# Folding the inverses into the keys of two recurrences

## The chip, the core and the metric

The kernel runs on one core of one Trainium2 chip. The metric is the device time of one execution in microseconds (us); lower is better. A core has TensorE (matmuls, with its weight loads), VectorE, ScalarE, GpSimd (POOL) and SyncE (SP, which here issues the DMAs). Each engine runs its instructions in a fixed order and waits on semaphores for the others.

## The reference, cut to what matters

One layer of a hybrid decoder: an input projection feeds four mixers (GLA, S5, gated delta net, RWKV-7), each is gated, and an output projection with a residual and a final norm follows. A prompt of 1024 tokens and 8 single tokens with carried states go through the same weights. All is in 32-bit floats. The change touches two mixers:

```python
# gated delta net, per head, chunks of 64 tokens
tmat = low + eye                       # unit lower triangular, 64x64
sol  = triangular_solve(tmat, concat([vb, kb * exp(gc)]))
u, w = sol[..., :64], sol[..., 64:]
def step(s, inp):                      # over chunks
    v_new = uu - ww @ s
    o = qd @ s + at @ v_new
    s = gt * s + kd.T @ v_new

# RWKV-7, per head, token by token
s = s * exp(lw_t) - (s @ kk_t)[..., None] * (kk_t * a_t) + v_t[..., None] * k_t
o = s @ r_t
```

The kernel computes RWKV in chunks of 64 as well, with the same kind of triangular inverse.

## The kernel before, in words

The prompt goes through in two halves of 512 tokens (`h` = 0, 1); the second carries the 8 single tokens as well. A half has two RWKV units and two delta-net units, one for each pair of heads (`rwkv_unit`, line 377; `gdn_unit`, line 616), two GLA units, S5 and eight gates. A unit is a generator with stages: projections; preparation (decays, keys, Gram matrices `Gt`); the inverses (`inverse`, line 288: eight chunks for two heads, a loop of 62 VectorE operations, DMAs through DRAM, small products); then the recurrence over eight chunks.

The string `ORDER` (line 33) lists the stages of all units in program order, and `PRI` (line 32) lets the recurrences and inverses of RWKV and delta net go ahead of the rest. The instructions of all engines are then put in order by a planner when the kernel is built, from modelled times (line 1553); each engine follows the order that it wrote. Weights are streamed by `stream` (line 270): SP loads a tile, ScalarE and POOL split it into a high and a low part, and TensorE makes three products for each of eight rows of the input (line 278). These projections are the bulk of TensorE's work and stand between the steps of the recurrences.

A step of RWKV (lines 466 to 502) handles one chunk for two heads. `AR[:, c]` holds 64 columns of keys (`ua`) and 64 of receptances (`vk`). In a bank `pc` it adds the value part (`Gt` times values, line 488) and `AR` times the state `Sbd` (line 489); VectorE copies the key half to `r` (line 491); `XT`, the inverse, times `r` (line 494) is copied into `UV` (line 495); `Bn` times `UV` (line 496) updates the state (line 501). So the chain has three products: state, inverse, update. Delta net (lines 674 to 705) has the same chain: `KQ` times state (693), `r` by adding the scaled values `Rv` (695), `XT` times `r` (697), the copy `U` (698), `Kn` times `U` (699) and the state update (704). For each pair of chunks some transposes come first (lines 472 to 478, 680 to 684).

Buffers come from pools that rotate (`NB`, line 25): nine `ta`, six `kA` (which hold `AR`, `BK`, `KQ`, the Gram matrices of delta net and GLA, and the rows of x while `norm_x` runs), two PSUM banks `psb` and three `psc`.

Of the kernel before, what the change touches and what calls it, by code (L numbers as in the profile page):

```python
# [8 lines left out]
F32 = mybir.dt.float32  # L9
# [3 lines left out]
ALU = mybir.AluOpType  # L13
# [17 lines left out]
           rU="V", dU="V", fg="V", la="V", tlo="V", cv0="V")  # L31
# [32 lines left out]
def trunk(ctx: ExitStack, tc: tile.TileContext, I, O):  # L64
    nc = tc.nc
    V, A, G, PE, SP = nc.vector, nc.scalar, nc.gpsimd, nc.tensor, nc.sync
# [33 lines left out]
    def psb(*shape):  # L100
        return ps_b.tile(list(shape) or [128, 512], F32, tag="b", name="psb")

    def psc(*shape):
        return ps_c.tile(list(shape) or [128, 512], F32, tag="c", name="psc")

    def ta(*shape, name="ta"):
        return tmp.tile(list(shape) or [128, NH], F32, tag="ta", bufs=NB["ta"], name=name)
# [11 lines left out]
    def cp(name, out, in_, scale=None):  # L119
        if ENG[name] == "A":  # L120
            return A.copy(out, in_) if scale is None else act(out, in_, AF.Copy, scale=scale)
        if scale is None:
            return V.tensor_copy(out, in_)
        return V.tensor_scalar(out, in_, scale, None, ALU.mult)
# [20 lines left out]
    ident = cload("ident", (128, 128))  # L145
# [9 lines left out]
    i64 = cload("i64", (128, 64))  # L155
# [176 lines left out]
    inner = lambda ap: ap.rearrange("p (c f) (b t) -> p c (f b) t", f=2, b=2)[:, :, 1:3, :]  # L332
    HS = [slice(64 * h, 64 * h + 64) for h in range(2)]
    outs, gp = {}, {}
    dgp = drp.tile([8, 128, HALF], F32, name="dgp")
    dy = drp.tile([HALF, D], F32, name="dy")

    def ou_tile(m, pair, h):
        outs[m, pair, h] = un.tile([128, 4, 128], F32, tag="on", bufs=NB["on"], name=f"on{m}{pair}")
        return outs[m, pair, h]  # L340
# [36 lines left out]
    def rwkv_unit(h, pair, th):  # L377
# [71 lines left out]
        if h:  # L449
# [11 lines left out]
            SP.dma_start(out=O["rwkv_s"][pair], in_=S0)  # L461
            sample_out(mat_vec(S0, rx[:, q]), RWKV, pair)
        yield
        ou = ou_tile(RWKV, pair, h)
        V.tensor_scalar(Sbd, Sbd, fx[:, 0, 0:1], None, ALU.mult)
        for c in range(8):
            if c % 2 == 0:
                Bn = tmp.tile([128, 2, 128], F32, tag="Bn", bufs=NB["Bn"], name="Bn")
                UV = tmp.tile([128, 2, 128], F32, tag="UV", bufs=NB["UV"], name="UV")
                pt = psc(128, 4, 128)  # L470
                for j in range(2):
                    PE.transpose(pt[:, j, :], BK[:, c + j, :], ident)
                vt = [vx[:, 64 * (c + j):64 * (c + j) + 64] for j in range(2)]
                PE.matmul(pt[64:128, 2, :], vt[0], ident, start=True, stop=True)
                PE.transpose(pt[0:64, 3, :], vt[1], ident)
                A.copy(Bn, pt[:, 0:2, :])
                A.copy(UV[64:128, 0], pt[64:128, 2])
                A.copy(UV[0:64, 1], pt[0:64, 3])  # L478
            uv, bn = UV[:, c % 2, :], Bn[:, c % 2, :]
            ua, vk = HS[c % 2], HS[1 - c % 2]  # L480
            gc = lambda rows, e: Gt[c // 4][rows, c // 2 % 2 * 4 + 2 * e + c % 2]
            pc = psc()

            def mm(o, l, r, start=False):
                PE.matmul(o, l, r, start=start, stop=True, skip_group_check=True)  # L485

            for e in range(2):
                mm(pc[:, HS[e]], gc(vk, e), uv[vk, HS[e]], start=(e == 0))
            mm(pc[:, 0:128], AR[:, c, :], Sbd)
            r = tmp.tile([128, 128], F32, tag="r", bufs=NB["r"], name="r")  # L490
            cp("rr", r[ua], pc[ua, 0:128])
            cp("rS", Sbd, Sbd, fx[:, 1, c:c + 1])
            for e in range(2):
                mm(pc[ua, 128 + 64 * e:192 + 64 * e], XT[ua, c // 2 * 2 + e, :], r[ua, HS[e]])
            cp("rU", uv[ua], pc[ua, 128:256])
            mm(pc[:, 256:384], bn, uv)
            for e in range(2):
                mm(pc[vk, HS[e]], gc(ua, e)[:, vk], uv[ua, HS[e]])
            for e in range(2):
                hp = HS[e]  # L500
                V.scalar_tensor_tensor(Sbd[hp, hp], pc[hp, 256 + 64 * e:320 + 64 * e], fx[hp, 1, c:c + 1], Sbd[hp, hp], ALU.mult, ALU.add)
            A.copy(ou[ua, c // 2, :], pc[vk, 0:128])
# [113 lines left out]
    def gdn_unit(h, pair):  # L616
# [42 lines left out]
        if h:  # L659
# [10 lines left out]
            SP.dma_start(out=O["gdn_s"][pair], in_=S0)  # L670
            sample_out(mat_vec(S0, qx[:, q]), GDN, pair)
        yield
        ou = ou_tile(GDN, pair, h)
        for c in range(8):
            if c % 2 == 0:
# [14 lines left out]
            def mm(o, l, r, start=False):  # L690
                PE.matmul(o, l, r, start=start, stop=True, skip_group_check=True)

            mm(pc[:, 0:128], KQ[:, c, :], Sbd, start=True)
            r = tmp.tile([128, 128], F32, tag="r", bufs=NB["r"], name="r")
            V.tensor_tensor(r[ua], pc[ua, 0:128], rv[ua], ALU.add)
            for e in range(2):
                mm(pc[ua, 128 + 64 * e:192 + 64 * e], XT[ua, c // 2 * 2 + e, :], r[ua, HS[e]])
            cp("dU", U[ua], pc[ua, 128:256])
            mm(pc[:, 256:384], kn[ua], U[ua])
            for e in range(2):  # L700
                mm(pc[vk, HS[e]], Gt[ua, c // 2 * 2 + e, 64:128], U[ua, HS[e]])
# [855 lines left out]
```

## Time and profile before

| | |
|---|---|
| median of 3 runs | 1058.57 us (1046.91 to 1059.12) |
| the profiled execution | 1059.9 us, of which the span of the trace is 1058.1 us |
| mean granted clock of TensorE | 0.854 of 2.4 GHz |
| TensorE busy | 929.8 us, 88% of the span |
| its weight loads | 764.5 us, 72% |
| VectorE busy | 698.9 us, 66% |
| ScalarE busy | 462.4 us, 44% |
| POOL busy | 391.1 us, 37% |
| DMA | 95.91 MB, mean 91 GB/s |

Busy time of an engine is the time in which at least one of its instructions runs. Matmuls are pipelined, so TensorE counts as busy while a single matmul is in flight. The granted clock is 1.00 at 2.4 GHz and 0.50 at 1.2 GHz. A product of 32-bit floats shows as two matmul records and two weight loads; a transpose, and a product of the projections, as one.

### The profile page before, as it was taken

The numbers are of one execution on the slowest core, as the hardware profiler recorded it, in microseconds if no ns is written. First come the engines' busy times: TensorE is split into PE (matmuls) and PEld (weight loads), VectorE is DVE, ScalarE is ACT, GpSimd is POOL, SyncE is SP. The second block draws the span as 40 slices with busy tenths as digits, with TensorE's granted clock in tenths as the row PEclk, the third lists the DMA queues.
The fourth block names the chain that finished last, engine by engine and source line by source line (L and its number), as shares of the span: only waits on it lengthen the run. The fifth ranks groups of instructions, "written<-read, shape, count | busy, mean of one in ns | idle before, by whom it ended". The sixth has DMA issues, their size and how long they took to land. (4 is left out here: it accounts for less than half of the span.)

```text
span 1058.1 us, 17042 instructions
## 1 busy us (share of the span) xinstructions
PE 929.8 (88%) x5994; PEld 764.5 (72%) x5994; DVE 698.9 (66%) x1843; ACT 462.4 (44%) x1088; POOL 391.1 (37%) x439
## 2 busy tenths in 40 slices
PE   3898989899998898797999989898998989897595
PEld 2676757678777686687788868777886968685594
DVE  8627895767548645836577979888976555725523
ACT  4355625331643423531663544554343354257233
POOL 2698654530221540015344513205523711432132
PEclk9999989975886866598999989868986969899697
DMA  7142423220220203125123332313121244437322
GB/s 234 56 143 77 137 74 81 80 60 5 77 63 28 81 29 120 58 64 160 50 81 96 100 91 80 92 27 85 33 62 40 83 132 132 147 117 240 139 80 91
DMA packets 85109, 95.91 MB, mean 91 GB/s; under 512 B 41640, under 2 KB 52016, under 8 KB 85024
## 3 DMA queue, kind: packets, MB, share of 16 engines
q1 hardware_dynamic: 85024, 94.83, 29.4%
q8 instruction: 47, 0.77, 0.3%
q14 instruction: 38, 0.31, 0.1%
HBM read 75.95 MB, written 16.72 MB: 88 GB/s over the span
## 5 line engine op out<-in xcount | busy, mean ns | idle before, releaser
L267 POOL TENSOR_TENSOR wl<-wr,wh 128x512 fp32r<-128x512 f32 x152 | 207.4, 1366 | 430.8 <-ACT wh L266 376.4
L278 PE MATMUL psp<-xhi,wh 128*128 128x260 f32 (+2 forms) x728 | 263.1, 362 | 4.8 <-DVE rx L357 2.2
L278 PE MATMUL psp<-xhi,wl 128*128 128x260 f32 (+2 forms) x728 | 254.0, 352 | 7.1 <-POOL wl L267 6.9
L278 PE MATMUL psp<-xlo,wh 128*128 128x260 f32 (+2 forms) x728 | 252.7, 348 | 0.7 <-DVE xlo L258 0.7
L278 PEld LDWEIGHTS psp<-xhi,wh 128*128 128x128 f32 x728 | 152.5, 209 | 26.4 <-issue 7.0
L278 PEld LDWEIGHTS psp<-xhi,wl 128*128 128x128 f32 x728 | 150.9, 208 | 26.3 <-POOL wl L267 10.9
L278 PEld LDWEIGHTS psp<-xlo,wh 128*128 128x128 f32 x728 | 152.6, 210 | 16.6 <-issue 4.4
L266 ACT CAST wh<-wr 128x512 fp32r<-128x512 f32 x152 | 93.6, 617 | 142.0 <-PE psp L278 73.5
L308 DVE TENSOR_TENSOR DP<-DT,LT 128x60 f32<-128x60 f32 (+24 forms) x248 | 76.2, 307 | 11.5 <-DMA LT<-d 5.5
L310 DVE TENSOR_TENSOR DT<-DT,DP 128x60 f32<-128x60 f32 (+24 forms) x248 | 77.0, 311 | 6.2
L278 PE MATMUL psp<-olo,wh 128*128 128x260 f32 (+1 forms) x192 | 64.5, 336 | 5.1 <-DVE olo L117 4.8
L278 PE MATMUL psp<-ohi,wh 128*128 128x260 f32 (+1 forms) x192 | 65.8, 345 | 3.4 <-ACT wh L266 1.9
L278 PE MATMUL psp<-ohi,wl 128*128 128x260 f32 (+1 forms) x192 | 63.8, 339 | 0.1
L278 PEld LDWEIGHTS psp<-olo,wh 128*128 128x128 f32 x192 | 38.3, 199 | 8.8 <-DVE olo L117 5.5
L278 PEld LDWEIGHTS psp<-ohi,wh 128*128 128x128 f32 x192 | 38.2, 200 | 6.9 <-ACT wh L266 2.3
L113 ACT ACTIVATE eg<-eg 128x260 f32<-128x260 f32 (+1 forms) x72 | 33.8, 485 | 18.7 <-DVE eg L200 18.2
L485 PE MATMUL psc<-UV,Gt 64*128 64x64 f32 (+1 forms) x256 | 39.8, 292 | 2.1 <-ACT UV L478 2.1
L278 PEld LDWEIGHTS psp<-ohi,wl 128*128 128x128 f32 x192 | 37.6, 198 | 3.0 <-POOL wl L267 0.4
L485 PEld LDWEIGHTS psc<-UV,Gt 64*128 64x128 f32 (+1 forms) x256 | 30.3, 189 | 11.5 <-issue 2.9
L117 POOL TENSOR_TENSOR df<-cum 128x256 f32<-128x256 f32 x48 | 30.4, 654 | 19.7 <-DVE cum L739 12.5
L764 PE MATMUL psb<-W 64*128 64x64 f32 x256 | 34.8, 319 | 0.1
L256 PE MATMUL psb<-constA,xn 128*128 128x128 f32 (+1 forms) x72 | 15.8, 375 | 20.3 <-DVE xn L252 9.9
(432 smaller groups left out, 1875.0 us busy)
## 6 DMA issues: line engine op xcount, KB each, us to landing
wr<-in_wct SPq DMA_DIRECT2D x120, 256.0 KB
wr<-in_wo SPq DMA_DIRECT2D x32, 256.0 KB
xn<-in_x SPq DMA_DIRECT2D x8, 512.0 KB
LT<-d SPq DMA_DIRECT2D x32, 128.0 KB
dgp<-gp SPq DMA_DIRECT2D x8, 256.0 KB
Gml<-dG SPq DMA_DIRECT2D x4, 512.0 KB
csT<-dph SPq DMA_DIRECT2D x4, 512.0 KB
dTl<-dT SPq DMA_DIRECT2D x4, 512.0 KB
```

The lines of the kernel that those rows point to most:

```text
L113: A.activation(out, in_, func, bias=bias, scale=scale, **kw)
L117: return (G if ENG[name] == "G" else V).tensor_tensor(out, a, b, op)
L256: PE.transpose(pt[:, k, :n], xn[:n, (4 * b + k) * 128:(4 * b + k + 1) * 128], ident[:n, :n])
L266: A.copy(hi, raw)
L267: G.tensor_tensor(lo, raw, hi, ALU.subtract)
L278: X["mm"] = PE.matmul(p[:, :m], w[:, k % 4, :], x[:, k, c0:c0 + m], start=(i == 0 and s == 0), stop=(i == 7 and s == 2))
L308: V.tensor_tensor(tp[:, :m, :w], DT[:, :m, j:j + 1].to_broadcast([128, m, w]), LT[:, j:j + 1, j + 1:32].to_broadcast([128, m, w]), ALU.mult)
L310: V.tensor_tensor(DT[:, :m, j + 1:32], DT[:, :m, j + 1:32], tp[:, :m, :w], ALU.add)
L485: PE.matmul(o, l, r, start=start, stop=True, skip_group_check=True)
L764: PE.matmul(pg[:, c, :], W[HS[e], t], W[HS[e], t].rearrange("p (b f s) -> p f b s", f=2, s=s)[:, 1], start=True, stop=True)
```

## The change

A new function `fold` multiplies the inverse into the keys, once per unit, before the recurrence starts. It transposes the key half of `AR` (or `KQ`) for eight chunks, four by a transpose and four by a product with the identity since they lie in the other half of the partitions, copies the result to `WT`, multiplies each 64x64 block by its inverse (sixteen products in two banks) and copies the blocks back over the keys. The state product then gives the inverse times keys times state at once, and `r` shrinks to the part that comes from the values: the inverse times `r` is put into the bank ahead of the state product and `U` is copied from the sum. In RWKV that `r` is made once per pair of chunks in `pt` (four products and one copy), and the value product of the step keeps the receptance half alone. In delta net `r` is `Rv` itself, so the addition goes, and a product with one column opens the other half of the bank.

```diff
+    def fold(W, XT):
+        WT = ta(128, 4, 128, name="WT")
+        pt = psb(128, 4, 128)
+        for c in range(0, 8, 2):
+            PE.transpose(pt[0:64, c // 2, :], W[:, c, 0:64], ident)
+        for c in range(1, 8, 2):
+            PE.matmul(pt[64:128, c // 2, :], W[:, c, 64:128], ident, start=True, stop=True)
+        A.copy(WT, pt)
+        for p in range(2):
+            pw = psb(128, 4, 64)
+            for b in range(4):
+                for e in range(2):
+                    PE.matmul(pw[HS[e], b, :], WT[HS[p], b, HS[e]], XT[HS[p], 2 * b + e, :], start=True, stop=True)
+            A.copy(W.rearrange("d (b p) s -> d p b s", p=2)[:, p, :, HS[p]], pw)
...
+        fold(AR, XT)
         ou = ou_tile(RWKV, pair, h)
...
+                r = tmp.tile([128, 128], F32, tag="r", bufs=NB["r"], name="r")
+                gc = lambda c, rows, e: Gt[c // 4][rows, c // 2 % 2 * 4 + 2 * e + c % 2]
...
-                PE.transpose(pt[0:64, 3, :], vt[1], ident)
+                PE.transpose(pt[0:64, 2, :], vt[1], ident)
                 A.copy(Bn, pt[:, 0:2, :])
                 A.copy(UV[64:128, 0], pt[64:128, 2])
-                A.copy(UV[0:64, 1], pt[0:64, 3])
+                A.copy(UV[0:64, 1], pt[0:64, 2])
+                for j in range(2):
+                    for e in range(2):
+                        PE.matmul(pt[HS[j], 3, HS[e]], gc(c + j, HS[1 - j], e)[:, HS[j]], UV[HS[1 - j], j, HS[e]], start=True, stop=True)
+                cp("rr", r, pt[:, 3])
...
             for e in range(2):
-                mm(pc[:, HS[e]], gc(vk, e), uv[vk, HS[e]], start=(e == 0))
+                mm(pc[ua, HS[e]], XT[ua, c // 2 * 2 + e, :], r[ua, HS[e]], start=(e == 0))
+            for e in range(2):
+                mm(pc[vk, HS[e]], gc(c, vk, e)[:, vk], uv[vk, HS[e]], start=(e == 0))
             mm(pc[:, 0:128], AR[:, c, :], Sbd)
-            r = tmp.tile([128, 128], F32, tag="r", bufs=NB["r"], name="r")
-            cp("rr", r[ua], pc[ua, 0:128])
             cp("rS", Sbd, Sbd, fx[:, 1, c:c + 1])
-            for e in range(2):
-                mm(pc[ua, 128 + 64 * e:192 + 64 * e], XT[ua, c // 2 * 2 + e, :], r[ua, HS[e]])
-            cp("rU", uv[ua], pc[ua, 128:256])
+            cp("rU", uv[ua], pc[ua, 0:128])
...
+        fold(KQ, XT)
         ou = ou_tile(GDN, pair, h)
...
-            mm(pc[:, 0:128], KQ[:, c, :], Sbd, start=True)
-            r = tmp.tile([128, 128], F32, tag="r", bufs=NB["r"], name="r")
-            V.tensor_tensor(r[ua], pc[ua, 0:128], rv[ua], ALU.add)
+            mm(pc[vk, 511:512], i64[ua], ident[ua, 0:1], start=True)
             for e in range(2):
-                mm(pc[ua, 128 + 64 * e:192 + 64 * e], XT[ua, c // 2 * 2 + e, :], r[ua, HS[e]])
-            cp("dU", U[ua], pc[ua, 128:256])
+                mm(pc[ua, HS[e]], XT[ua, c // 2 * 2 + e, :], rv[ua, HS[e]], start=(e == 0))
+            mm(pc[:, 0:128], KQ[:, c, :], Sbd)
+            cp("dU", U[ua], pc[ua, 0:128])
```

## Rows read from the trace of the kernel before

**Rows 1.** Page, busy us (share of the span) and instructions.

```profile
PE 929.8 (88%) x5994; PEld 764.5 (72%) x5994; DVE 698.9 (66%) x1843; ACT 462.4 (44%) x1088; POOL 391.1 (37%) x439
```

**Rows 2.** Windows: length, busy us (count) per engine, granted clock, DMA.

```profile
150.00:475.00 325.00, 298.60 (x1770) 234.26 (x1768) 206.39 (x582) 130.45 (x301) 88.78 (x101) 0.77 0.21 63
...
530.00:900.00 370.00, 343.56 (x2565) 293.24 (x2563) 284.13 (x741) 169.44 (x411) 129.50 (x148) 0.88 0.28 81
...
380.00:396.00 16.00, 16.00 (x100) 14.90 (x101) 6.84 (x17) 2.60 (x7) 4.53 (x5) 0.50 0.06 17
```

**Rows 3.** TensorE's waits: total us, times, longest.

```profile
PE psc L485 <- DVE state L501: 9.2, 9, 2.5
PE psc L691 <- DVE U L123: 7.2, 9, 1.6
...
PE psc L691 <- DVE r L695: 2.1, 4, 1.1
...
PE psc L485 <- DVE r L123: 0.8, 2, 0.4
```

**Rows 4.** Timeline, a delta-net step: start, length, engine, line, operation [idle].

```profile
399.31 0.80 PE L691 MATMUL psc<-state,KQ 128*128 128x128 f32 x2
...
400.15 0.28 DVE L695 TENSOR_TENSOR r<-psc,Rv 64x128 f32<-64x128 f32 x1 [0.17 <-PE psc L691]
...
400.49 0.69 PE L691 MATMUL psc<-r,XT 64*64 64x64 f32 x4 [0.38 <-DVE r L695]
...
401.36 0.27 DVE L123 COPY U<-psc 64x128 f32<-64x128 f32 x1
...
403.13 0.59 DVE L704 SCALAR_TENSOR_TENSOR state<-state,egb,psc 64x64 f32<-64x64 f32 x2 [0.41 <-PE psc L691]
...
403.78 0.80 PE L691 MATMUL psc<-state,KQ 128*128 128x128 f32 x2 [0.68 <-DVE state L704]
```

**Rows 5.** Timeline, VectorE: first and last of 16 state updates.

```profile
338.88 0.57 DVE L704 SCALAR_TENSOR_TENSOR state<-state,egb,psc 64x64 f32<-64x64 f32 x2
...
466.54 0.58 DVE L704 SCALAR_TENSOR_TENSOR state<-state,egb,psc 64x64 f32<-64x64 f32 x2 [1.50 <-PE psc L691]
```

**Rows 6.** SP's waits (us, times, longest), and SP's timeline there.

```profile
SPq L138 <- PE psc L691: 23.1, 2, 22.6
...
404.61 0.33 SPq L138 DMA_DIRECT2D xn<-in_norm_g  x1
```

**Rows 7.** Timeline, VectorE: a delta-net step at 2.4 GHz.

```profile
417.89 0.29 DVE L695 TENSOR_TENSOR r<-psc,Rv 64x128 f32<-64x128 f32 x1 [0.64 <-PE psc L691]
...
418.74 0.29 DVE L123 COPY U<-psc 64x128 f32<-64x128 f32 x1
```

**Rows 8.** Timelines of TensorE and groups of ScalarE: prices.

```profile
137.60 1.59 PE L654 MATMUL psb<-SK,raw 64*64 64x128 f32 x32 [3.64 <-ACT SK L632]
...
152.84 0.38 PE L472 MATMUL psc<-constA,BK 128*128 128x128 f32 x2
153.15 0.43 PE L474 MATMUL psc<-constA,rx 128*64 128x128 f32 x2
153.51 0.30 PE L475 MATMUL psc<-constA,rx 128*64 128x128 f32 x1
...
299.58 2.40 PE L654 MATMUL psb<-SK,raw 64*64 64x128 f32 x24
...
411.71 0.44 PE L691 MATMUL psc<-r,XT 64*64 64x64 f32 x4
412.08 0.50 PE L278 MATMUL psp<-xhi,wh 128*128 128x512 f32 x1
...
L476 ACT COPY Bn<-psc 128x256 f32<-128x256 f32 x16 | 5.9, 367 | 7.1 <-PE psc L475 7.1
...
L804 ACT COPY vn<-psb 128x512 f32<-128x512 f32 x4 | 2.3, 586 | 1.6 <-PE psb L803 1.6
```

**Rows 9.** Timeline, a weight load after another shape.

```profile
402.41 0.39 PEld L691 LDWEIGHTS psc<-U,Gg 64*64 64x64 f32 x3 [0.22 <-issue]
```

More of the change, by code (lines that the diff above doesn't have):

```diff
@@ L474, in rwkv_unit @@
                 PE.matmul(pt[64:128, 2, :], vt[0], ident, start=True, stop=True)
-                PE.transpose(pt[0:64, 3, :], vt[1], ident)
+                PE.transpose(pt[0:64, 2, :], vt[1], ident)
                 A.copy(Bn, pt[:, 0:2, :])
                 A.copy(UV[64:128, 0], pt[64:128, 2])
-                A.copy(UV[0:64, 1], pt[0:64, 3])
+                A.copy(UV[0:64, 1], pt[0:64, 2])
[3 more added lines that the diff above has]
+                cp("rr", r, pt[:, 3])
             uv, bn = UV[:, c % 2, :], Bn[:, c % 2, :]
             ua, vk = HS[c % 2], HS[1 - c % 2]
-            gc = lambda rows, e: Gt[c // 4][rows, c // 2 % 2 * 4 + 2 * e + c % 2]
             pc = psc()
@@ L487, in rwkv_unit @@
             for e in range(2):
-                mm(pc[:, HS[e]], gc(vk, e), uv[vk, HS[e]], start=(e == 0))
+                mm(pc[ua, HS[e]], XT[ua, c // 2 * 2 + e, :], r[ua, HS[e]], start=(e == 0))
+            for e in range(2):
+                mm(pc[vk, HS[e]], gc(c, vk, e)[:, vk], uv[vk, HS[e]], start=(e == 0))
             mm(pc[:, 0:128], AR[:, c, :], Sbd)
-            r = tmp.tile([128, 128], F32, tag="r", bufs=NB["r"], name="r")
-            cp("rr", r[ua], pc[ua, 0:128])
             cp("rS", Sbd, Sbd, fx[:, 1, c:c + 1])
-            for e in range(2):
-                mm(pc[ua, 128 + 64 * e:192 + 64 * e], XT[ua, c // 2 * 2 + e, :], r[ua, HS[e]])
-            cp("rU", uv[ua], pc[ua, 128:256])
+            cp("rU", uv[ua], pc[ua, 0:128])
             mm(pc[:, 256:384], bn, uv)
             for e in range(2):
-                mm(pc[vk, HS[e]], gc(ua, e)[:, vk], uv[ua, HS[e]])
+                mm(pc[vk, HS[e]], gc(c, ua, e)[:, vk], uv[ua, HS[e]])
             for e in range(2):
```

## The prediction

> **What bounds the kernel now.** I read the busy table of the page first. TensorE holds 88% of the span [rows 1], so the question is whether it is kept busy by work or by waiting. The second view cuts the span into the two stretches in which the recurrences of RWKV and delta net run, one for each half of the prompt. There TensorE has a matmul in flight for 298.60 of 325 us and 343.56 of 370 us [rows 2], 92% together. It has little idle time to give back, 53 us in both. But its granted clock is only 0.77 and 0.88, that is, for some 34% of those 695 us it ran at 1.2 GHz and not at 2.4 (weighted mean 0.83).
>
> The third view is TensorE's list of waits. The waits that the recurrences cause are for the state (9.2 us in the longest row) and for U (7.2 us); those for `r`, which the change takes away, are 2.1 us and 0.8 us [rows 3]. So the wait that goes is the smallest of the three in a step, because the planner has put other products there.
>
> The fourth view is one step by itself, with nothing between. At 1.2 GHz it is state product 399.31, `r` 400.15, inverse product 400.49, U copy 401.36, state update 403.13, next state product 403.78: 4.47 us [rows 4]. In the stream, however, steps are twice as far apart: from the first to the last of the 16 state updates of delta net in the first half, 338.88 to 466.54, it is 8.51 us each [rows 5]. So the chain is about 4.47/8.51 = 0.53 of a step; the rest is other work that stands between in the engines' orders.
>
> There is one place where the chain decides more than that. The load of `norm_g` for the second half sits in SP's queue behind a buffer that the last product of the first delta-net unit frees; SP stood 22.6 us for it, with the next weight loads queued behind [rows 6]. From 380 to 396 us TensorE had no projections, only small products, and was granted 0.50 though it was never idle [rows 2].
>
> **The change part by part.** *Shorter chain.* With the inverse already in the keys, the U copy can start where `r` starts now. That is 401.36 - 400.15 = 1.21 us less per step at 1.2 GHz [rows 4] and 418.74 - 417.89 = 0.85 us at 2.4 GHz [rows 7]; mixed 34 to 66, 0.97 us, and for 64 steps 62 us. The inverse product itself stays, on other data (`r` of values alone), ahead of the state product and off the chain. Off this comes what the fold puts on the chain of each unit, once the inverse is there: eight products (0.8 us by the price below), one copy of 0.37 us as `Bn` [rows 8], some 0.2 us between engines, 1.4 us, 11 us in eight units. Net 51 us. If the chain is on the path for 0.53 of the time, the span gets **-27 us**; the ends are 0 (other work fills the same time) and -51 (the chain sets everything).
>
> *Fold on TensorE.* Per unit four transposes, four products with the identity, sixteen of 64x64. Two transposes took 0.31 us, so 0.62 for four; one identity product (two records) 0.36 us, so 1.44; sixteen 64-deep products (32 records) that alternate between column halves, as the fold's do, took 1.59 us [rows 8]. Sum 3.65 us, in eight units 29 us at 2.4 GHz. Had the sixteen to go one behind the other like the two inverse products in one column half (0.37 us for two [rows 8]), they would take 2.96 us, and the eight units 40; I take the lower, since the alternation is the same as in its row.
>
> *More products per step.* RWKV gets two calls more (the value part goes ahead into `pt`, for both chunks of a pair; its old one is narrowed from 128 to 64 columns), delta net one (the one-column product that opens the bank). At 0.1 us (1.59/16) that is 6.4 + 3.2 = 9.6 us; the ends are 0 and 0.185 us each, 18. Together 39 us at 2.4 GHz; at 1.2 GHz twice that (24 records took 2.40 us [rows 8], double per record); with 34% at the lower clock 52 us. In the 92% in which TensorE is taken it lengthens the span: **+48 us**. The ends are 0 (the 53 us of idle time could take it all) and +72 (all at 1.2 GHz: 78 x 0.92).
>
> *Vector engine.* Delta net loses 32 additions and RWKV 16 of its 32 copies of `r`; 48 x 0.28 us [rows 4] = 13.4 us. It is busy for 206.39 of 325 us and 284.13 of 370 [rows 2], and steps stand behind its other work; I count half, **-7 us** (ends 0 and -13).
>
> *Scalar engine.* Three more copies per unit, 0.586 + 2 x 0.367 us [rows 8], 10.6 us in all. It is busy for 130.45 of 325 us [rows 2], so I cost this at nothing; without that cover it would be 10.6 us.
>
> *Buffers.* WT takes one of the nine `ta` and each unit three passes through the two `psb` banks. The trace has no such wait; by the copies that hold a bank it is between 0 and 8 x 1.3 = 10 us, and I take 0, because the planner can place them while other units run. No DMA is added, and neither SP's nor POOL's queue gets an instruction.
>
> Sum: 48 - 27 - 7 = **+14 us** on the profiled execution of 1059.9 us: 1074. That execution lies 1.3 us over the median of the three runs (1058.57), so as a median 1072 us, 1.3% up.
>
> Behind the switch from one shape to another TensorE's weight loader stood 0.22 us with nothing to wait for [rows 9]. The Trainium skill (TensorEngine Tiling (Array Packing), Key Properties) says that a change of tiling mode, unlike a change of tile, drains the engine; this speaks against the fold, which adds some four such changes per unit. By it the sum would be 8 x 4 x 0.22 = 7 us higher, 1079; I leave it out of the forecast, because the row of the sixteen products and the identity product already begin behind such a change.
>
> **The rivals.** *The chain sets the end (faster).* The place is the first half's end: delta net's first unit ends sooner, SP's queue moves on sooner, weights come, and the stretch from 380 us is filled with projections at 2.4 GHz. For it: the 22.6 us [rows 6] and the clock of 0.50 with nothing but small products [rows 2]. Against: 92% busy. It decides if more than about 0.8 of the chain's 51 us lies on the path and half of the new products fall into holes: -51 + 24 - 7 = -34, 1025 us as a median.
>
> *The new products pull the clock down (slower).* Small products and low clock go together in the trace: 16.00 of 16 us busy at 0.50 [rows 2]. If the folds, which have priority over the projections, bring the same, all added work runs at 1.2 GHz (+72) and the shorter chain only opens room that other work already filled (at most -27, say -20): 72 - 20 - 7 = +45, 1104 us. It decides once the mean clock of the two stretches falls to 0.80 or below. The Trainium skill (TensorE: Matmul & The Clock Gate, Part 1) says the opposite of what this needs: idling throttles the engine and activity releases it. By that the added products would hold 2.4 GHz and cost 39 x 0.92 = 36 us, the sum +2, 1061 us; the 0.50 row, where the engine was never idle, doesn't bear that out for runs of small products, so this end gets one chance in ten.
>
> *The change doesn't shorten what it means to.* The order of all engines is planned anew from modelled times, and the value products may be put right in front of the U copy, where they delay it by as much as the inverse product did. Then only the price is left, +48 - 7, within the slow rival.
>
> **How the numbers follow.** The forecast case (1061 to 1085) gets 0.42, the fast rival 0.24, the slow one with the last 0.23, and the clock that holds 0.11. For this kernel, 2% is 1037 to 1080. Faster takes nine tenths of the fast rival, 0.22; slower the slow one and a fifth of the forecast case, 0.32; within 2% is the rest, 0.46. With a tenth left out at either end the range is 1026 to 1103 us; the forecast case's own is 1061 to 1085.
>
> **What would show it.** Right: TensorE has about 190 small products more for the folds (by calls), its busy time is up by 30 to 60 us, a step by itself goes from 4.5 to about 3.3 us at 1.2 GHz, the spacing of the delta-net updates falls from 8.5 to some 7.5 us, vector busy time falls by 13 us. Wrong on the gain: the spacing stays at 8.5, or SP's wait for the last delta-net product of the first half stays at 20 us. Wrong on the price: TensorE's busy time hardly rises, or the mean clock of the two stretches goes above 0.88. What would overturn it all is a new order in which projections run out in another place than now.

## The result, and the profile after

The changed kernel takes 1112.19 us (median of 4 runs, 1107.66 to 1113.32) and the kernel before 1058.67 on the same chip: a ratio of 1.0519, 95% interval 1.0472 to 1.0566. The span of the profiled execution is 1105.9 us, 47.8 more than before, at a mean granted clock of 0.847 (before 0.854). That is slower, and above my range of 1026 to 1103. Ratios here and below are taken over the fast runs of each kernel and are not the quotients of the medians.

The page's busy times, which answer to [rows 1]:

```profile
PE 945.9 (86%) x6538; PEld 772.7 (70%) x6538; DVE 691.6 (63%) x1795; ACT 472.5 (43%) x1112; POOL 391.7 (35%) x439
```

TensorE is busy for 16.1 us more, so two thirds of the 47.8 us is time in which it has nothing in flight: span less busy time goes from 128.3 to 160.0.

The windows of the recurrences (columns as in [rows 2]). The first ends earlier than before, 441 us against 475; the second later, 943 against 900.

```profile
150.00:441.00 291.00, 266.60 (x1894) 204.74 (x1894) 195.92 (x545) 126.80 (x295) 86.26 (x96) 0.81 0.22 64
530.00:943.00 413.00, 351.12 (x2753) 296.29 (x2752) 280.20 (x716) 172.40 (x417) 125.41 (x144) 0.82 0.24 70
```

The chain itself became as short as meant. In TensorE's and VectorE's timeline, the U copy starts 0.83 us after the state product at 1.2 GHz (first pair) and 0.53 us at 2.4 GHz (second); before it was 401.36 - 399.31 = 2.05 us [rows 4], and at 2.4 GHz 418.74 - 417.40 = 1.34, its state product standing in the first line of the second fence, of before.

```profile
398.27 0.79 PE L713 MATMUL psc<-state,KQ 128*128 128x128 f32 x2 [1.98 <-ACT KQ L351]
399.10 0.28 DVE L123 COPY U<-psc 64x128 f32<-64x128 f32 x1
...
367.49 0.49 PE L713 MATMUL psc<-state,KQ 128*128 128x128 f32 x2
368.02 0.29 DVE L123 COPY U<-psc 64x128 f32<-64x128 f32 x1 [0.78 <-PE psc L713]
```

```profile
417.40 0.46 PE L691 MATMUL psc<-state,KQ 128*128 128x128 f32 x2 [1.21 <-DVE state L704]
...
896.54 0.59 DVE L704 SCALAR_TENSOR_TENSOR state<-state,egb,psc 64x64 f32<-64x64 f32 x2 [1.93 <-PE psc L691]
```

VectorE's delta-net state updates after: the first and last of the first half, and the last of the second.

```profile
335.07 0.56 DVE L726 SCALAR_TENSOR_TENSOR state<-state,egb,psc 64x64 f32<-64x64 f32 x2
...
438.96 0.57 DVE L726 SCALAR_TENSOR_TENSOR state<-state,egb,psc 64x64 f32<-64x64 f32 x2 [1.15 <-PE psc L713]
...
939.29 0.59 DVE L726 SCALAR_TENSOR_TENSOR state<-state,egb,psc 64x64 f32<-64x64 f32 x2
```

The spacing in the first half is (438.96 - 335.07)/15 = 6.93 us, before 8.51, and its last update comes 27.6 us earlier than in [rows 5]. In the second half the last update comes 42.8 us later (896.54 before). So the loss arises in the second half. The stretches there, cut at 574 us (where the second RWKV unit's preparation stands before; after, it comes only at 604), at the end of RWKV and at the end of delta net, all engines before and after, and then the projections of line 278 alone, before (from 441 us) and after (from 439):

```profile
574.00:753.00 179.00, 163.36 (x1273) 138.96 (x1271) 156.41 (x428) 88.55 (x209) 59.77 (x67) 0.88 0.27 75
753.00:897.00 144.00, 134.50 (x954) 112.98 (x952) 94.14 (x250) 57.70 (x151) 48.50 (x49) 0.83 0.28 84
```

```profile
574.00:756.00 182.00, 139.26 (x1134) 114.11 (x1133) 129.24 (x362) 76.27 (x179) 32.13 (x37) 0.77 0.21 57
756.00:940.00 184.00, 166.18 (x1267) 139.85 (x1266) 113.34 (x292) 72.52 (x188) 67.13 (x73) 0.81 0.25 75
```

```profile
441.00:574.00 133.00, 81.56 (x550) 73.98 (x550) 0.92 0.31 94
574.00:753.00 179.00, 89.98 (x566) 79.67 (x564) 0.88 0.27 75
753.00:897.00 144.00, 60.08 (x343) 50.01 (x343) 0.83 0.28 84
```

```profile
439.00:574.00 135.00, 94.79 (x623) 83.98 (x624) 0.91 0.32 98
574.00:756.00 182.00, 57.28 (x361) 51.65 (x360) 0.77 0.21 57
756.00:940.00 184.00, 75.24 (x469) 63.50 (x470) 0.81 0.25 75
```

Read the counts of projections. Up to 574 there are 73 more than before (623 against 550): that is what became of the shorter first half. From there to the end of RWKV there are 205 fewer (361 against 566), yet the stretch is no shorter (182 against 179 us); TensorE idles for 42.7 us of it (before 15.6), POOL, which splits the weights, is busy for 32 us and not 60, and the clock is 0.77 and not 0.88. From the end of RWKV to the end of delta net 126 of them are made up, and that stretch is 40 us longer. So RWKV waited while little was put beside it, and the delta net then had that work to do as well. What RWKV waited for most shows in TensorE's waits:

```profile
PE psi L324 <- DVE Dn L319: 26.9, 4, 14.6
PE psc L508 <- DVE state L522: 10.7, 9, 3.0
...
PE psc L713 <- DVE state L726: 8.2, 9, 3.1
PE psp L278 <- DVE gp L1242: 8.1, 4, 4.7
```

The first is the inverse's small product; before, its row had 1.2 us. Two of its waits, 10.64 us up to 592.41 and the longest, 14.6, up to 707.36, are nearly all of the 27 us that the stretch idles more. In the timeline the second unit's preparation (line 406) came only after the first unit's fold (line 350), at 603.52; before, it ran at 574.20. The two use the same two `psb` banks.

```profile
592.41 1.06 PE L324 MATMUL psi<-Dn,Gt 32*32 32x32 f32 x16 [10.64 <-DVE Dn L319]
595.43 1.12 PE L350 MATMUL psb<-XT,WT 64*64 64x64 f32 x16 [0.45 <-ACT XT L328]
...
603.52 1.23 PE L406 MATMUL psb<-rx,constB 64*128 64x260 f32 x2
...
707.36 1.06 PE L324 MATMUL psi<-Dn,Gt 32*32 32x32 f32 x16 [14.61 <-DVE Dn L319]
```

```profile
574.20 1.14 PE L389 MATMUL psb<-rx,constB 64*128 64x260 f32 x4
```

### The profile page after: what moved, and what is told of

The parts are those of the page before. It is cut to its first block, busy times and chain, and to the rows that moved or that the text cites. A ratio compares the mean times of both kernels' runs of the same rounds, so it can differ in the third digit from the quotient of the medians.

```text
span 1105.9 us, 18118 instructions
## 1 busy us (share of the span) xinstructions
PE 945.9 (86%) x6538; PEld 772.7 (70%) x6538; DVE 691.6 (63%) x1795; ACT 472.5 (43%) x1112; POOL 391.7 (35%) x439
## 5 line engine op out<-in xcount | busy, mean ns | idle before, releaser
L278 PE MATMUL psp<-xhi,wh 128*128 128x260 f32 (+2 forms) x728 | 257.9, 355 | 12.6 <-DVE gp L1242 8.1
L278 PE MATMUL psp<-xhi,wl 128*128 128x260 f32 (+2 forms) x728 | 252.3, 351 | 4.2 <-POOL wl L267 4.0
L278 PE MATMUL psp<-xlo,wh 128*128 128x260 f32 (+2 forms) x728 | 249.0, 343 | 0.9 <-DVE xlo L258 0.9
L278 PEld LDWEIGHTS psp<-xhi,wh 128*128 128x128 f32 x728 | 149.5, 205 | 35.6 <-DVE gp L1242 9.4
L278 PEld LDWEIGHTS psp<-xhi,wl 128*128 128x128 f32 x728 | 148.1, 205 | 24.6 <-POOL wl L267 6.9
L278 PEld LDWEIGHTS psp<-xlo,wh 128*128 128x128 f32 x728 | 149.6, 206 | 15.6 <-issue 3.2
L310 DVE TENSOR_TENSOR DT<-DT,DP 128x60 f32<-128x60 f32 (+24 forms) x248 | 73.9, 298 | 6.7
L278 PE MATMUL psp<-olo,wh 128*128 128x260 f32 (+1 forms) x192 | 64.7, 337 | 6.1 <-DVE olo L117 5.2
L278 PE MATMUL psp<-ohi,wh 128*128 128x260 f32 (+1 forms) x192 | 65.4, 342 | 1.7 <-ACT ohi L1291 1.5
L278 PE MATMUL psp<-ohi,wl 128*128 128x260 f32 (+1 forms) x192 | 63.8, 338 | 0.2 <-POOL wl L267 0.2
L278 PEld LDWEIGHTS psp<-olo,wh 128*128 128x128 f32 x192 | 38.4, 200 | 10.0 <-DVE olo L117 6.2
L278 PEld LDWEIGHTS psp<-ohi,wh 128*128 128x128 f32 x192 | 38.0, 199 | 4.9 <-ACT ohi L1291 1.8
L278 PEld LDWEIGHTS psp<-ohi,wl 128*128 128x128 f32 x192 | 37.8, 199 | 2.7 <-POOL wl L267 0.4
L786 PEld LDWEIGHTS psb<-W 64*128 64x128 f32 x256 | 30.9, 221 | 7.8 <-POOL W L117 2.7
L374 DVE SCALAR_TENSOR_TENSOR rx<-psp,imu,sh 128x260 f32<-128x260 f32 (+2 forms) x22 | 12.2, 553 | 33.9 <-ACT sh L113 33.7
L609 DVE SCALAR_TENSOR_TENSOR acc<-raw,constA,acc 128x512 f32<-128x512 f32 x36 | 30.2, 866 | 5.0 <-ACT acc L113 5.0
```

Source lines behind the costliest of these rows:

```text
L278: X["mm"] = PE.matmul(p[:, :m], w[:, k % 4, :], x[:, k, c0:c0 + m], start=(i == 0 and s == 0), stop=(i == 7 and s == 2))
L310: V.tensor_tensor(DT[:, :m, j + 1:32], DT[:, :m, j + 1:32], tp[:, :m, :w], ALU.add)
L374: V.scalar_tensor_tensor(out[:, c0:c0 + m], p, imu[:, ct:ct + 1], sh[:, c0:c0 + m], ALU.mult, ALU.add)
L609: V.scalar_tensor_tensor(acc[:, :HALF], raw[:, j:j + HALF], w(j), acc[:, :HALF], ALU.mult, ALU.add)
L786: PE.matmul(pg[:, c, :], W[HS[e], t], W[HS[e], t].rearrange("p (b f s) -> p f b s", f=2, s=s)[:, 1], start=True, stop=True)
```

## The experiments

Three causes were open: the banks that the fold holds (the preparation waits for them), the added work itself, and the order that the planner makes, in which both are only symptoms. The expectations call them theories H, P and O. Ratios are to the kernel before on the same chip, with 95% intervals.

### Banks or work: four parts of the change

`fold_psi`: the change with the fold's products in the bank of the inverse's products.

```diff
-            pw = psb(128, 4, 64)
+            pw = ps_i.tile([128, 4, 64], F32, tag="i", name="psi")
```

> The changed kernel, but the sixteen products of each fold go through the PSUM bank of the inverse (pool ps_i) and not through the two psb banks; same work, same shorter chain. Theory H (the fold's psb banks, taken in program order ahead of the next unit's preparation, stand held until the inverse is there, so the preparation of the second RWKV unit of the second half comes some 27 us late): the products of L406 for that unit run before the first inverse products of the second half, the 10.6 us and 14.6 us waits of L324 for Dn go, the first half keeps its 27 us gain; 1030 to 1050 us, ratio to before 0.97 to 0.99. Theory P (the loss is TensorE's price for the fold and the extra products): the same work is there, so 1100 to 1115. Theory O (any new order loses against the one that before happened to have): 1080 to 1115.

`hold_only`: the kernel before, with two passes through `psb` per unit, each one small product of `XT`, and no fold.

```diff
+    def hold(XT):
+        for p in range(2):
+            pw = psb(128, 4, 64)
+            PE.matmul(pw[0:64, 0, :], XT[HS[p], 0, :], XT[HS[p], 0, :], start=True, stop=True)
+            junk = tmp.tile([128, 128], F32, tag="r", bufs=NB["r"], name="r")
+            A.copy(junk[0:64, 0:64], pw[0:64, 0, :])
...
+        hold(XT)
```

> The kernel before, with nothing of the change but two passes through psb at the place of the fold: one 64x64 product of the inverse and a small copy each, the results unused. Theory H: 32 records of product in all are under 3 us of TensorE, but the second half shows the hole of the changed kernel (first inverse product of the second half ahead of the second unit's preparation products, that unit's inverse loop some 25 us later) and has no shorter chain to set against it: 1085 to 1125. Theory P: 1057 to 1065. Theory O: anything from 1057 to 1100, but without that hole in particular.

`fold_work`: the kernel before, with all of the fold's products and copies, through the bank `psi`, copied back into `WT` and not used.

```diff
+            A.copy(WT[:, 2 * p:2 * p + 2, :], pw.rearrange("q (a b) s -> q a (b s)", a=2))
...
+        fold(AR, XT)
...
+        fold(KQ, XT)
```

> The kernel before with all the fold's products and copies (through the inverse's bank, results written to the fold's own tile and unused), the steps as before: price of the fold without hold and without the shorter chain. Theory H: TensorE's 25 us of fold products lengthen it by 5 to 30 us: 1064 to 1090. Theory P: as long as the changed kernel or longer, 1100 to 1120.

`first_half`: the change for `h` = 0 alone.

```diff
+NEW = {"R": (1, 0), "D": (1, 0)}
...
+        new = NEW["R"][h]
+        if new:
+            fold(AR, XT)
```

> The change in the first half of the prompt only (fold through psb and the step with two products); the second half's units have the steps of before. Theory H: the first half's gain of 27 us (last delta-net update 439 and not 467 us) is kept and the second half has no hold: 1025 to 1045. Theory P: half of the price, 1075 to 1090. Theory O: 1060 to 1110.

Measured: `fold_psi` 1111.64 us, 1.0534 (1.0446 to 1.0621); `hold_only` 1100.82, 1.0405 (1.0336 to 1.0474); `fold_work` 1080.74, 1.0189 (1.0093 to 1.0284); `first_half` 1071.97, 1.0152 (1.0079 to 1.0225).

So a kernel with hardly any added work loses 4%, and one with all of the fold's work 2% (its interval reaches from 0.9 to 2.8): the loss doesn't go by the work. That looked like the banks. But in `fold_psi`, which takes the fold's products out of `psb` and leaves its transposes there, the loss stayed whole, and the wait for the inverse moved into the first half (22 us, up to 227 us). Its list of TensorE's waits begins:

```profile
PE psi L324 <- DVE Dn L319: 26.0, 3, 22.0
```

And `first_half`, which had only the half that gained, ended behind the kernel before.

### The control for the banks

`hold_one` makes the two passes in one unit only, the RWKV unit whose passes had stood before the late preparation. `pass_early` makes them in every unit, but of `AR` and `KQ`, which are there before the inverse is, so that nothing waits in a bank.

```diff
+        if h and pair == 1:
+            hold(XT)
```

```diff
+            PE.matmul(pw[0:64, 0, :], W[HS[p], 0, 0:64], W[HS[p], 0, 0:64], start=True, stop=True)
...
+        hold(AR)
...
+        hold(KQ)
```

> The kernel before with the two psb passes of one tiny product of the inverse at one place only: in the first RWKV unit that runs in the second half (two products, two small copies in the whole kernel, results unused). Theory H (the loss is made where that unit's psb tiles, ahead in the rotation of the next unit's preparation, wait for the inverse): the second unit's preparation products move from 574 to 600 us or later and the whole takes 1075 to 1100. Theory P (TensorE's price) and theory G (the gain of the first half is hidden elsewhere and nothing more): two products cost nothing, 1055 to 1064.

> The control to the run with two psb passes in every unit (1101 us): the same passes, products of the same size and copies, but fed by the keys (AR, KQ), which are there before the inverse is. Theory H: no bank stands held, the second unit's preparation stays at 574 to 590 us, and the whole is 1055 to 1070. If the passes themselves, or any new order, cost the time: 1085 to 1105 as before.

`fold_psc` is the change with the fold's products in the `psc` banks, and `delta_only` the change in delta net alone.

```diff
-            pw = psb(128, 4, 64)
+            pw = psc(128, 4, 64)
```

```diff
+NEW = {"R": (0, 0), "D": (1, 1)}
```

> The changed kernel with the sixteen products of each fold in the three psc banks, which only the recurrences' own steps and later products use, in place of the two psb banks (through the inverse's bank the first half got a hold of its own, since there the next unit's inverse comes ahead of the fold in that bank). Theory H: neither half has a hold; the first half keeps its 27 us and the second half's RWKV steps their 20 us, of which what other work hides is lost: 1035 to 1075. Theory P: 1100 to 1115.

> The change in the delta-net units alone, RWKV as before. Theory H: the fold of delta net takes its psb banks after the second RWKV unit's preparation and so doesn't hold it: 1050 to 1075, and most of the loss belongs to RWKV's fold. Theory P: delta net has four of the eight folds and half of the extra products, so half of the loss, about 1085.

Measured: `hold_one` 1094.55, 1.0345 (1.0284 to 1.0407); `pass_early` 1090.82, 1.0312 (1.0251 to 1.0374); `fold_psc` 1090.48, 1.0314 (1.0248 to 1.0379); `delta_only` 1091.18, 1.0328 (1.0257 to 1.0399). The second unit's preparation in the timeline of `hold_one`, and then of `pass_early`:

```profile
599.62 2.10 PE L396 MATMUL psb<-rx,constB 64*128 64x260 f32 x4
```

```profile
584.21 1.14 PE L396 MATMUL psb<-rx,constB 64*128 64x260 f32 x4
```

The control has the preparation 15 us earlier, 10 us later than before, and loses the same 3%. With that the hold by a late inverse fell as the main cause: it is there, but four kernels with quite different edits land within some 4 us of each other. They have in common that all of their instructions were put in order anew, and also that each takes more passes through the two `psb` banks than the kernel before; these two aren't told apart here.

### Moving the preparation back, and edits without work

`swap_after` is the change with two neighbours of `ORDER` exchanged, so that the preparation comes ahead of the fold in program order; `swap_after_psc` has the `psc` banks as well. `before_replan1` and `before_replan2` are the kernel before with not one instruction added or removed: an entry of `ORDER` three places earlier, and one priority halved.

```diff
-M' R1' R0' D0' g5
+M' R0' R1' D0' g5
```

```diff
-R0' g2 R1' g3 M' R1' R0' D0'
+R0' g2 R1' R0' g3 M' R1' D0'
```

```diff
-PRI = {"R2": 4000,
+PRI = {"R2": 2000,
```

> The changed kernel with two neighbouring entries of ORDER exchanged, so that the second RWKV unit of the second half is prepared ahead of the first one's fold in program order (same work; in the kernel before the same exchange changes nothing but two rows of TensorE's order). Theory H (the held psb banks ahead of that preparation are a cause of the loss): the preparation products move from 604 back to 580 to 595 us, the hole after 581 us goes, 1065 to 1095. Theory O (any new plan loses some 15 to 45 us against the plan that before has): 1075 to 1105, whatever becomes of that hole. Theory P (TensorE's price): 1105 to 1115.

> The same exchange, and the fold's products in the psc banks (1090 us without the exchange). Theory H: nothing is held there already, so the exchange gains at most 10 us: 1075 to 1095. Theory O: a fresh draw, 1070 to 1110.

> The kernel before with its work unchanged to the last instruction, and only a new plan: the second RWKV unit of the second half is prepared two entries earlier in ORDER. Theory O: the same work in a new order loses as the others did, 1070 to 1100. Theories H and P: nothing is held and nothing is added, 1050 to 1065.

> The kernel before with its work unchanged, planned with half the priority of the inverse stage (R2 2000 in place of 4000). Theory O: 1070 to 1100. Theories H and P: 1050 to 1070.

Measured: `swap_after` 1103.15, 1.0443 (1.039 to 1.0497); `swap_after_psc` 1094.51, 1.0371 (1.0314 to 1.0428); `before_replan1` 1065.71, 1.0088 (1.0044 to 1.0131); `before_replan2` 1070.39, 1.0111 (1.0035 to 1.0187). In `swap_after` the preparation is back at 575.42 and the wait for the inverse is gone from the top of the list, but only 9 us come back by the medians, and the two intervals still overlap. In `swap_after` the last RWKV update comes at 741.48 us and the last of delta net at 926.84. Its stretches cut there, all engines and then the projections alone:

```profile
574.00:742.00 168.00, 141.31 (x1176) 116.26 (x1174) 131.00 (x380) 79.17 (x189) 37.02 (x39) 0.85 0.25 68
742.00:928.00 186.00, 168.72 (x1213) 142.39 (x1214) 100.41 (x272) 62.63 (x165) 63.24 (x69) 0.72 0.16 47
...
574.00:742.00 168.00, 70.22 (x447) 62.12 (x445) 0.85 0.25 68
742.00:928.00 186.00, 63.61 (x376) 55.70 (x377) 0.72 0.16 47
```

RWKV now takes 168 us, 11 fewer than before, but again with too little beside it (447 projections against 566, POOL 37.02 us against 59.77), and the delta net pays: 186 us for 144, this time at a clock of 0.72. And an edit with no work at all costs about 1%: neither of the two neighbouring orders reaches that of the kernel before. It is less than the 1070 to 1100 us that I expected if the order alone made the loss (1065.71, and 1070.39 at its lower end).

### One kernel's work in the other's order

This test separates work from order best. In `new_work_old_order` the changed computation is held in the order that the kernel before has on each engine, by ordering edges between instructions that both have; the new ones, the state products and the small copies at the head of a pair of chunks find their own place between them. For that the fold goes through `psc`, its second part is done within the first two steps, `WT` has a buffer of its own (`sh` 1 and not 2), and the value products stand ahead of the inverse product. `psc_halves` is that same kernel without the edges. `old_work_new_order` holds the work of the kernel before in the order of the changed one (with the fold's buffers and the one-column product left in as place holders).

```diff
+    for text in PINS:
...
+            ins = nc.find_inst_by_name(f"I-{n}")
...
+            if last is not None:
+                tc.add_manual_dep(ins, last.name, info, reason="pin")
+            last = ins
```

> The changed kernel's work in the order of the kernel before: on each engine all instructions that both kernels have (4242 of TensorE's 4306 products left after taking out the ones the change moves; 1748 of VectorE, 952 of ScalarE, all of GpSimd and SP) are held in before's sequence by ordering edges; the new ones, the state products and the small copies at the head of a pair of chunks find their own place. The fold goes through psc in two halves and has its own buffer, so that no bank of the preparation is held. Theory O (the plan makes the loss): the price alone is left, 9 us of TensorE work and some copies, 1060 to 1080. Theory P (the work makes the loss): 1095 to 1115.

> The kernel before's work (three products in the chain of a step, no fold) in the order of the changed kernel, held on all five engines in the same way; only delta net's one-column product, which opens a bank early, is kept of the change, and the fold's tiles are allotted and not used. Theory O: the loss comes with the order, 1090 to 1120. Theory P: 1058 to 1072.

> The control to the first: the same kernel (fold through psc in two halves, own buffer) without the ordering edges, planned anew. Theory O: 1075 to 1105, above the same work in before's order by 15 or more. Theory P: the same as with the edges, within 10.

Measured: `new_work_old_order` 1059.78, 1.0023 (0.9975 to 1.0071); `psc_halves` 1073.32, 1.0129 (1.0088 to 1.017); `old_work_new_order` 1196.43, 1.1273 (1.1191 to 1.1356). The first one's page, and then windows of its two stretches:

```profile
PE 922.3 (87%) x6538; PEld 761.2 (72%) x6538; DVE 681.1 (65%) x1795; ACT 471.7 (45%) x1112; POOL 394.2 (37%) x439
```

```profile
574.00:749.00 175.00, 158.64 (x1427) 135.57 (x1426) 148.65 (x405) 91.45 (x219) 60.77 (x67) 0.88 0.28 76
749.00:895.00 146.00, 137.64 (x1040) 117.56 (x1039) 89.41 (x232) 58.69 (x155) 48.03 (x49) 0.84 0.27 83
```

It has the instructions of the changed kernel (x6538, x1795, x1112) and the stretches of the kernel before (175 and 146 us against 179 and 144, POOL 60.77 against 59.77). So the added work and the shorter chain together cost nothing that can be measured, -0.3 to +0.7%; no run has the one without the other in the old order. The changed kernel does the same work and loses 5%, so it is not the work that makes the loss.

How much the order makes is another question, and here the control counts. `psc_halves` has the same instructions and buffers as `new_work_old_order` and only lacks the edges. On the same work the planner's own order thus costs 13.5 us, 1.1% by the ratios, clear of noise but less than the 15 or more that I expected. The rest, some 40 us between `psc_halves` (1.0129) and the changed kernel (1.0519), goes with what was altered to hold the old order at all (the fold's banks, the buffers, the place of the value products), together with the plan that each form gets, and no run separates these. One rival fits all the times and wasn't tested: every kernel that takes more passes through `psb` than the one before, and is planned anew, loses 1.5 to 5.3%, while the three planned anew without a further pass (`before_replan1`, `before_replan2`, `psc_halves`) lose 0.9 to 1.3% (at the meeting ends, `first_half` and `fold_work`, the intervals overlap). So it can be the passes through these two rotating banks, early or late, that force the bad orders.

The other corner agrees in sign, and shows where the order hurts; its waits:

```profile
PE psi L333 <- DVE Dn L328: 26.9, 4, 13.7
PE psc L495 <- DVE state L511: 21.2, 15, 5.1
PE psc L702 <- DVE state L716: 11.6, 12, 2.4
```

The 26.9 us in all for the inverse are as many as in the changed kernel (the longest wait is 13.7 us and not 14.6). Its 12.7%, above the 1090 to 1120 us that I expected, can't be put down to the order alone, since an order planned for the short chain here meets the long one; and the fold's `psb` tiles are allotted in it too, so it doesn't tell the banks from the order.

### Can the shorter chain pay at all?

`free_rec` is `new_work_old_order` with the recurrences left free to move. `half1_free` and `half1_old` plan the first half anew and keep the second half's order, the one with free steps there, the other without. The edit in all three is a shorter list of edges.

```diff
-PINS = (
...
+PINS = (
...
```

> The changed kernel's work in before's order, but the recurrences of RWKV and delta net free to find their own place (4050 of TensorE's products held, none of a step). If the shorter chain has a gain that only the held order hid (theory G), the steps close up and it shows: 1035 to 1050. If the steps stand between other work anyway and the chain is not on the path (theory N), 1052 to 1066, like the wholly held order (1060).

> As that, but only what belongs to the second half of the prompt (from its norm on, with what the first half leaves over) is held in before's order; the first half is planned anew for the changed kernel, as in the run where its last delta-net update came at 436 us (465 in before). Theory G: that gain of 27 to 30 us passes on, since the second half keeps before's order: 1030 to 1045. Theory N: it is taken up in front of the second half, where S5's products and the preparation stand in a fixed sequence: 1050 to 1066.

> As the one before, with the second half's steps held as well. Theory G: 1032 to 1048, the first half's gain alone. Theory N: 1052 to 1068.

Measured: `free_rec` 1067.07, 1.0061 (1.0028 to 1.0094); `half1_free` 1065.9, 1.0045 (1.0017 to 1.0073); `half1_old` 1064.15, 1.0027 (0.9992 to 1.0061). In `half1_old` the last delta-net update of the first half, and the first projection of the second half; then that projection before, and in the changed kernel:

```profile
435.41 0.57 DVE L740 SCALAR_TENSOR_TENSOR state<-state,egb,psc 64x64 f32<-64x64 f32 x2 [0.94 <-PE psc L727]
...
453.38 0.59 PE L287 MATMUL psp<-xhi,wh 128*128 128x260 f32 x1 [3.03 <-DVE gp L1256]
...
447.84 0.58 PE L278 MATMUL psp<-xhi,wh 128*128 128x260 f32 x1 [0.40 <-DVE gp L1220]
...
440.58 0.57 PE L278 MATMUL psp<-xhi,wh 128*128 128x260 f32 x1
```

The update is 31 us earlier than in [rows 5], and the second half's first projection 5.5 us later than before (447.84). The projection waits for other work, here for the tile `gp` that VectorE writes, not for the recurrence. In the changed kernel the second half's projections do begin earlier, but by 7.3 us (447.84 to 440.58) and not by 27.6. So the first half's gain is real and ends in nothing in `half1_old`: the recurrence's last product isn't what lets the second half begin. No version that I ran beats the kernel before.

## Why the prediction was wrong

**What failed.** The sum was made as if the planner's order were a constant: each term was priced in the order of before, and the plan made anew was treated as free ("the planner can place them while other units run"). My last sentence named what would overturn it, a new order in which projections run out in another place, and that happened, from 574 to 756 us; but it had no case, no price and no chance. A term for it belonged in the sum: on the changed work a new plan measured +13.5 us (`psc_halves` against `new_work_old_order`), neutral edits of the kernel before +0.9 and +1.1%, the smallest edits with a pass through a bank +3 to +4%, all slower. It would have moved the forecast up by 10 to 40 us and the weight to slower.

**Fold and extra products, +48: mis-sized.** TensorE is busy for 16.1 us more, below the 30 to 60 that I named as the sign of a right price. The fold was priced at 29 us at 2.4 GHz, which is 39 with 34% at the lower clock; its groups by line, with busy time behind the bar, sum to 25.6. The price of the sixteen products came from a row whose products have 128 columns, and the fold's have 64: one such group took 0.98 us, and not 1.59 (last line; the granted clock from 394 to 396.4 us was 0.92).

```profile
L350 PE MATMUL psb<-XT,WT 64*64 64x64 f32 x256 | 10.5, 248 | 1.3 <-ACT XT L328 0.9 <-ACT WT L345 0.4
...
L713 PE MATMUL psc<-constA,constB 64*64 64x1 f32 x64 | 9.4, 215 | 0.2
...
L344 PE MATMUL psb<-constA,KQ 128*64 128x128 f32 x32 | 5.4, 316 | 0.0
L344 PE MATMUL psb<-constA,AR 128*64 128x128 f32 x32 | 4.4, 279 | 0.0
...
395.32 0.98 PE L350 MATMUL psb<-XT,WT 64*64 64x64 f32 x32 [0.35 <-ACT WT L345]
```

(The transposes of line 342 add 2.4 and 2.9 us, and one of the lines, the one-column product, belongs to the steps.) What was wrong besides is the step from busy time to span, the factor of 0.92. `new_work_old_order` has all of that work in a span 2.8 us shorter than before, and its TensorE is busy for 922.3 us, less than the 929.8 before. It also had a clock of 0.868 for 0.854, and part of that is paid back so: less time at 1.2 GHz, (0.146 - 0.132)/0.5 of 1057 us = 30 us, saves at most 15 us of busy time. Added work of at most some 7 us at equal clock is an estimate from these. So the lower end, 0 ("the 53 us of idle time could take it all"), was near the value, as far as the sum of work and chain shows it.

**Shorter chain, -27: right in mechanism, nothing in the span.** Per step 1.22 us at 1.2 GHz (2.05 - 0.83) and 0.81 at 2.4 (1.34 - 0.53), where I had 1.21 and 0.85. The spacing fell further than I wrote, to 6.93 us, and SP's long wait for the last delta-net product went from 22.6 us [rows 6] to 6.8:

```profile
SPq L138 <- PE psc L713: 8.2, 2, 6.8
```

But of the 27.6 us at the end of the first half none reaches the end of the kernel, and `half1_old` shows this with the order of the second half held. The share of 0.53 of a step was measured rightly and used wrongly: that the chain fills half of a step says nothing on whether the last step releases anything. My other end, 0, was the value there.

**Vector and scalar engine.** VectorE's busy time fell by 7.3 us (13 priced, 7 counted) and ScalarE's rose by 10.1 (10.6 priced). `new_work_old_order` has the same ScalarE work at no cost in the span, so it was covered as said.

**Buffers, 0 with an end of 10: put at nothing without a reason.** "The planner can place them while other units run" had no row behind it. The fold's passes did stand ahead of the preparation, which moved from 574 to 604 us. Taking that away (`swap_after`) gave 9 us of 53; but the passes stayed, and the form without any (`psc_halves`) lies some 40 us under the changed kernel. How much of these 40 is the banks stays open.

**The rule left out.** The 7 us for the fold's changes of tiling mode were kept out of the forecast. `new_work_old_order` has the fold's changes of mode and stands at 1.0023; its interval reaches from -2.6 to +7.5 us for all of the added work and the shorter chain together, so a separate charge of 7 isn't borne out, nor excluded.

**The rivals.** The fast one named a place that did change: from 380 to 396 us the clock is 0.79 where it was 0.50, and the DMA share 0.44 where it was 0.06. But the stretch didn't fill with projections, and the span gained nothing (above).

```profile
380.00:396.00 16.00, 15.65 (x138) 13.64 (x139) 9.74 (x21) 5.39 (x11) 4.48 (x4) 0.79 0.44 147
...
380.00:396.00 16.00, 0.96 (x3) 0.49 (x3) 0.79 0.44 147
```

(The second line is the projections alone.) The slow one gave 1104, near the time, but by another mechanism: it needed the added products to pull the clock down, with the mean of the two stretches at 0.80 or below. It is (291 x 0.81 + 413 x 0.82)/704 = 0.816 after, and with the same products in the old order the whole kernel's clock is higher than before, 0.868. So the number of small products doesn't set it. In the stretch from 574 us, where it fell most, there were also fewer projections (361 against 566); that these are the reason is not shown. That the time came near 1104 is luck. The third, the value products delaying the U copy, is excluded by the 0.83 and 0.53 us.

**Open.** How much of the loss is the order as such, and how much the passes through `psb`, isn't separated beyond the 13.5 us: the changed kernel's own banks were never held in the old order, nor were idle passes through `psb` put into the kernel before with its order held. Which places of the new order cost how much isn't separated: the wait for the inverse, RWKV's missing projections and the low clock come in different mixtures in `fold_psi`, `swap_after` and the changed kernel. Whether an order exists in which the shorter chain pays wasn't settled; the whole change was run in ten versions.

## What to carry to other kernels

When a planner orders the engines, an edit changes two things, the work and the draw of the order, and the second can be the larger: hold one version's work in the other's order, with the same buffers in both, run that form without the hold as well, and replan the unchanged kernel with neutral edits, before a difference is put down to the edit. Give the new order a term and a chance in the forecast, on the slow side if neutral edits of the kernel are slower too. And a shorter chain pays only if its last product releases something: follow what starts next, and what that waits for, before the saved time is counted.

## What the runs showed of the hardware

TensorE can be in flight all the time and yet be granted the lower clock. In the changed kernel this 25 us window has it busy for 25.00 us at a granted clock of 0.51, in the delta-net stretch of the second half; 23 of its 157 records are projections (`L278`, the second line), the rest other, mostly small products:

```profile
800.00:825.00 25.00, 25.00 (x157) 22.14 (x157) 8.99 (x22) 4.48 (x11) 6.71 (x8) 0.51 0.12 30
...
800.00:825.00 25.00, 6.62 (x23) 5.19 (x23) 0.51 0.12 30
```

The Trainium skill (TensorE: Matmul & The Clock Gate, Part 1) has the throttled state as the default that activity releases. This window, like the one in [rows 2] at 380 us, doesn't agree with that if activity means being in flight.

A product with a single column has a record of 215 ns on average (line 713 above), hardly less than one with 64 columns (248 ns, line 350); both groups mix the two clocks. Records of neighbours overlap: the 64 records of the first cover 9.4 us in all, 147 ns each, and the 256 of the second 10.5 us, 41 ns each. What the single column adds to a step is not shown.
